# Prompt attention of a two-layer decoder step in two passes over the heads, with half of the output projection issued among the second pass

## The chip, the core and the metric

The kernel runs on one core of one Trainium2 chip. The metric is the device time of one execution in microseconds (us), taken as the median of three runs. Before the change it is 2921.13 us, and the three runs lie between 2912.52 and 2928.78 us.

A core has five engines that each work through a list of instructions of their own, in its order: PE (TensorE: matrix products, and transposes as products with an identity), DVE (VectorE), ACT (ScalarE), POOL (GpSimd) and SP, which here only issues transfers. An instruction waits at the head of its engine's list until what it needs is there, and everything behind it on that engine waits too.

## What is computed

The kernel is one inference step of a decoder of two layers: a gated linear attention layer, then a layer with differential attention, each followed by an MLP with squared ReLU. It works on a prompt of 1024 tokens (with 16 "meta" tokens ahead) and on 8 running sequences of which one token each is added ("the samples"). The change touches the attention of the prompt in the second layer and the projection behind it. Cut to that, the reference is:

```python
q, k, v = diff_project(x, w_in, pos)             # 8 heads; q and k have 2 maps of 64, v has 128
s = einsum('bqhmd,bkhmd->bhmqk', q, k) * 64**-0.5
s = where(k_pos[None, :] <= q_pos[:, None], s, -inf)
p = softmax(s, axis=-1)
a = p[:, :, 0] - lam * p[:, :, 1]                # the two maps of a head, subtracted
o = einsum('bhqk,bkhe->bqhe', a, v)
o = rms_norm(o, g_sub) * (1.0 - lam_init)        # over the 128 elements of a head
f = o.reshape(B, T, 1024) @ w_out                # w_out is 1024 x 1024
x = layer_norm(ALPHA * x + f)                    # post_norm, then the MLP
```

Everything is float32. A query sees all keys up to its own position, so that the later tokens have more keys.

## The kernel before

**Precision.** A product of two float32 matrices is made of three matmuls of a rounded type. Each operand is split into a high part and a low part: `split` (L181) copies the operand into the high part on ACT (L182) and subtracts it from the original on DVE (L183). `mm3` (L185) adds high x high, high x low and low x high (L186, L187, L188). Weights are split by `unit` and `kunit` (L162 to L179): SP loads pieces of 128 x 512 into a pool of two raw tiles, ACT rounds them into the high part (L173), GpSimd subtracts for the low part (L174). The two parts lie in the tiles `whi` and `wlo`, two of each. `kunit(w, c0)` does that for 256 columns of a 1024 x 1024 matrix, in four pieces; one such quarter of `w_out` is a unit `u`.

**Accumulators.** Results of PE go to PSUM, into three pools: `mmt` (three banks of 512 columns: the scores, `w_out`), `axt` (three banks: transposes) and `smt` (two banks: the product with V, the samples).

**Order.** Each engine's list is fixed when the kernel is built. A scheduler makes it, which takes the order in which the program issues the work as priority, and a model of the durations. So an instruction that the program issues earlier mostly stands earlier in its engine's list, but it may also be moved past others.

**Attention.** There are eight heads; a head has eight tiles of 128 queries, t = 0 to 7, and tile t has W = 16 + 128(t+1) keys.

- `prep(h)` (L1112 to L1157) makes a head's operands. It loads its 1024 keys, 1024 queries, the meta keys and the values; the raw data lie in `wlo` and `whi`, the tiles of the weights, so that two heads' are there at once. It transposes K and Q (17 transposes: one of 16 rows, eight of K, eight of Q) and splits them (four splits of 512 columns, one of 16). For every head after the first, nine transfers on GpSimd's queue (L1150 to L1156) then stack the high and the low part of each map's 64 rows, so that all 128 partitions are used and two matmuls (L1178, L1179) do the work of three; head 0 uses three (L1174 to L1176). The operands lie in half h%2 of `XH` and `XL`, the two big tiles that elsewhere hold the features of the tokens, high and low part; each half is for 512 tokens.
- `tile_(h, t)` (L1159 to L1202) computes one tile. For each map and each chunk of at most 512 keys PE makes the scores, and DVE (L1182) scales and masks them on the way out of PSUM and keeps a running row minimum (of the negated scores). ACT exponentiates (L1184) and sums; DVE combines the two maps (L1186 to L1188). PE transposes the result by 128 keys (L1197), ACT copies it out of PSUM (L1199), and PE multiplies with V (L1202) into a quarter of an `smt` bank.
- Four tiles share that bank. When it is full, ACT copies it to `Y` and squares it, and DVE sums the squares (L1239).
- `o_norm` (L1206 to L1214) normalizes finished heads, two at a time: DVE and GpSimd make the factor, and the multiplication (L1214) is GpSimd's, except for head 7, where DVE does it. `o_fm(h, c)` (L1216 to L1222) transposes head h of 512 tokens (c = 0 or 1) and splits the result into `XH` and `XL`, for `w_out`.

The loop (L1225 to L1250) runs over the heads once. `prep(h + 1)` is issued ahead of the first tile of head h, that is, one head ahead. The tiles come in the order 7, 1, 5, 3, 6, 0, 4, 2. Head 7 has 3, 2, 1, 0, 7, 6, 5, 4: after its tile 0 the first 512 tokens are finished, and `o_fm(j, 0)` for all heads j is issued ahead of its last four tiles. After the loop come `o_fm(j, 1)` and, in the next stage, eight loads of the residual (L1259 to L1261).

**Projection.** `w_out` (L882 to L908) goes through eight steps (u, c), a quarter of the columns of `w_out` for half of the tokens, in the order (0,0), (1,0), (0,1), (1,1), (2,0), (3,0), (2,1), (3,1). A step fills two accumulators, each by 48 matmuls of 256 columns, and DVE adds each to the residual in `Y` (L900). `w_out` is a generator: it hands on (`yield`) each pair of a token tile and half of its columns when it is ready, and `normalize` (L918 to L942) takes them from it, makes the layer norm and, after each half of the tokens, calls `to_fm` (L944 to L958), which transposes them for the MLP. Amid `w_out` the products of the samples (`samples`, from L1300; matmuls at L506) are issued. The MLP begins behind it (L1502).

## Time and profile before

The table is from the profiled execution, whose span, from its first to its last instruction, is 2919.7 us; the time of an execution is about 1 us more than its span. Stages are told apart by which lines run in them.

| | us |
|---|---|
| median of three runs (2912.52 to 2928.78) | 2921.13 |
| span of the profiled execution | 2919.7 |
| first row minimum of attention | 1814.3 |
| first matmul of the last group with V, and its duration | 2087.38, 1.28 |
| first matmul of the MLP | 2195.04 |
| mean granted clock of TensorE | 0.976 |

Matmuls are pipelined, and the recorded duration of one holds time in which the next is already running; the busy time of PE is therefore the time in which at least one was under way, and says nothing of how closely they follow each other. How often one can follow the next is read from the starts in a timeline. For DVE, ACT and GpSimd, busy time is time of work, except where an instruction is held up while it runs.

In the rows of groups, the columns are line, engine, operation, result and operands with their shapes and the count, then the busy time of the group and the mean ns of one instruction, then the idle time ahead of it and what ended that. In a timeline they are start, duration, engine, line and operation. In a table of stretches they are the stretch and its length, then the busy time and the number of instructions of PE, its weight loads, DVE, ACT and GpSimd, then the granted clock, the busy share of the DMA engines and GB/s.

### The profile page before, as it was taken

To read this page: it belongs to the slowest core of one execution; us is meant where nothing else is said; L and a number is where in the kernel's file an instruction comes from. 1 tells how busy PE (TensorE), PEld (TensorE's weight loads), DVE (VectorE), ACT (ScalarE), POOL (GpSimd) and SP (SyncE) were. 2 spreads that over 40 slices of the span, in tenths; PEclk is the share of its full clock that TensorE was granted. 3 is DMA by queue.
4 is the path that set the end of the run, shared out by engine and by line. 5 is a ranking of instruction groups with operands and counts; after the bars stand their busy time and mean duration, and the time that the engine had idled before them with its cause. 6 is when DMAs were issued, how large, how long until landed. Compare 5 with 4: busy or idle time off the path is not lost. (4 is left out here: it accounts for less than half of the span.)

```text
span 2919.7 us, 52085 instructions
## 1 busy us (share of the span) xinstructions
PE 2779.7 (95%) x19653; PEld 2277.6 (78%) x19653; DVE 1891.2 (65%) x2982; ACT 1044.1 (36%) x2075; POOL 1133.7 (39%) x867
## 2 busy tenths in 40 slices
PE   8889999999999999999999998889998999999997
PEld 5666767987777777777898896778888889797885
DVE  2564644457877777777667942788638855838478
ACT  3233453251222122122321112667524535335352
POOL 2230222233333334334233331132335766677664
PEclk9899999999999999999999998999999999999998
DMA  7557651514798988988387999363436778595893
GB/s 257 178 185 251 233 177 37 198 56 141 242 350 297 335 309 298 346 317 321 137 275 252 348 343 314 75 139 86 119 112 205 195 207 232 152 281 129 257 246 87
DMA packets 285366, 636.46 MB, mean 218 GB/s; under 512 B 25510, under 2 KB 141292, under 8 KB 273852
## 3 DMA queue, kind: packets, MB, share of 16 engines
q1 hardware_dynamic: 252716, 520.66, 51.6%
q0 software_dynamic: 32400, 112.50, 15.9%
q8 instruction: 154, 2.52, 0.4%
q14 instruction: 96, 0.79, 0.1%
HBM read 575.55 MB, written 44.06 MB: 212 GB/s over the span
## 5 line engine op out<-in xcount | busy, mean ns | idle before, releaser
L174 POOL TENSOR_TENSOR wlo<-raw,whi 128x512 fp32r<-128x512 f32 x256 | 360.0, 1419 | 744.0 <-ACT whi L173 670.8
L186 PE MATMUL mmt<-whi,XH 128*128 128x256 f32 (+1 forms) x1760 | 527.4, 302 | 2.9 <-ACT Y L310 2.0
L187 PE MATMUL mmt<-wlo,XH 128*128 128x256 f32 (+1 forms) x1760 | 527.8, 301 | 0.7 <-POOL wlo L174 0.7
L186 PE MATMUL mmt<-XH,whi 128*128 128x512 f32 (+1 forms) x1216 | 438.1, 361 | 7.4 <-DVE HL L183 7.2
L188 PE MATMUL mmt<-whi,XL 128*128 128x256 f32 x1536 | 437.2, 286 | 0.1
L188 PE MATMUL mmt<-XH,wlo 128*128 128x512 f32 (+1 forms) x1216 | 434.4, 358 | 0.0
L790 DVE TENSOR_REDUCE sc<-pg 128x16 f32<-128x1024 f32 x256 | 309.7, 1214 | 93.4 <-POOL pg L789 90.1
L173 ACT CAST whi<-raw 128x512 fp32r<-128x512 f32 x256 | 152.9, 619 | 578.4 <-PE mmt L188 191.1
L186 PEld LDWEIGHTS mmt<-whi,XH 128*128 128x128 f32 x1760 | 333.4, 190 | 30.1 <-issue 15.6
L187 PEld LDWEIGHTS mmt<-wlo,XH 128*128 128x128 f32 x1760 | 334.8, 190 | 28.2 <-issue 16.8
L187 PE MATMUL mmt<-XL,whi 128*128 128x512 f32 x768 | 307.3, 400 | 0.0
L188 PEld LDWEIGHTS mmt<-whi,XL 128*128 128x128 f32 x1536 | 292.1, 191 | 9.9 <-issue 8.8
L789 DVE TENSOR_TENSOR pg<-pg,qb 128x1024 f32<-128x1024 f32 x192 | 256.8, 1343 | 62.1 <-DMA pg<-in_cache_k 38.1
L186 PEld LDWEIGHTS mmt<-XH,whi 128*128 128x128 f32 x1216 | 231.7, 191 | 55.1 <-issue 13.7
L789 POOL TENSOR_TENSOR pg<-pg,qb 128x1024 f32<-128x1024 f32 x64 | 158.6, 2478 | 293.5 <-DMA pg<-in_cache_k 236.7
L188 PEld LDWEIGHTS mmt<-XH,wlo 128*128 128x128 f32 x1216 | 231.8, 191 | 35.8 <-issue 3.8
L186 PE MATMUL mmt<-whi,HH 128*128 128x512 f32 x512 | 205.6, 402 | 1.7 <-DVE Y L1014 1.7
L187 PE MATMUL mmt<-wlo,HH 128*128 128x512 f32 x512 | 204.7, 400 | 0.0
L188 PE MATMUL mmt<-whi,HL 128*128 128x512 f32 x512 | 203.9, 398 | 0.0
L187 PEld LDWEIGHTS mmt<-XL,whi 128*128 128x128 f32 x768 | 145.4, 189 | 39.6 <-issue 8.8
L1416 POOL TENSOR_TENSOR wlo<-RW,whi 128x512 fp32r<-128x512 f32 x96 | 156.3, 1749 | 37.1 <-ACT whi L1415 37.0
L1416 POOL TENSOR_TENSOR wlo<-rw,whi 128x512 fp32r<-128x512 f32 x92 | 147.7, 1674 | 41.4 <-ACT whi L1415 41.2
(441 smaller groups left out, 5769.3 us busy)
## 6 DMA issues: line engine op xcount, KB each, us to landing
pg<-in_cache_k SPq DMA_DIRECT2D x256, 512.0 KB, 6.0
pg<-in_cache_v SPq DMA_DIRECT2D x256, 512.0 KB, 6.0
XH<-xc POOLq DMA_DIRECT2D x42, 1032.0 KB, 7.9
raw<-in_mlp_w SPq DMA_DIRECT2D x164, 256.0 KB, 3.5
swt<-in_mlp_w SPq DMA_DIRECT2D x32, 1024.0 KB, 5.6
rw<-in_mlp_w SPq DMA_DIRECT2D x116, 256.0 KB, 3.8
RW<-in_mlp_w POOLq DMA_DIRECT2D x96, 256.0 KB, 6.0
xc<-XH POOLq DMA_DIRECT2D x14, 1032.0 KB, 6.8
```

What stands on the lines that cost most here:

```text
L173: S.copy(hi[:, c], raw)
L174: G.tensor_tensor(lo[:, c], raw, hi[:, c].bitcast(F32), op=ALU.subtract)
L186: TE.matmul(ps, ah, bh, start=first, stop=False)
L187: TE.matmul(ps, ah, bl, start=False, stop=False)
L188: TE.matmul(ps, al, bh, start=False, stop=last)
L789: eng.tensor_tensor(pg, pg, qb, op=ALU.mult)
L790: return V.tensor_reduce(sc[:, n, :], pg.rearrange("p (h d) -> p h d", d=64), op=ALU.add, axis=AX.X).ins
L1416: G.tensor_tensor(lo[:, k, :], t, hi[:, k, :].bitcast(F32), op=ALU.subtract)
```

## The change

The loop over the heads is run twice. The first pass computes tiles 0 to 3 of all heads, in the order 3, 1, 2, 0, and the second tiles 4 to 7, in the order 7, 5, 6, 4.

- `prep(late, h)` is called for each pass: in the first it loads 528 keys and the first 512 queries, in the second all 1040 keys, again, and the last 512 queries. In the first pass it is issued two heads ahead, in the second one head ahead. The nine transfers are now made 15 times instead of seven.
- Operands have new places (`places`): in the first pass the halves of `XH` and `XL` in turn and a new tile `opb`; in the second `XH`'s half 1 and `opb` in turn, since half 0 of `XH` and `XL` then holds the finished first 512 tokens. The low part of K has a tile of its own, `klt`. The raw data of the second pass lie in the space of `XL`'s half 1 (`araw`), so that `whi` and `wlo` are free for weights; `XL`'s half 1 is taken anew behind the last head.
- Between the passes `o_norm` and `o_fm(j, 0)` finish the first half, the residual of its tokens is loaded, and `w_out` is begun for c = 0 alone, `paced`: it stops after each accumulator. After the second tile of each head of the second pass it is taken one accumulator further, 48 matmuls and the addition on DVE. What it hands on is kept in `finished`.
- Behind the second pass a second call of `w_out` does (0,1), (1,1), (2,1), (3,1), for which the four units are loaded and split again. `both` hands the kept pairs and those of the second call to `normalize`.
- The pool of probabilities (`scp`) is as wide as the pass needs, with five tiles in the first and four in the second; `aT`'s pool is opened for each pass, with six tiles. There are three tiles of meta values instead of two. `o_norm` is called ten times instead of six, on half as many tokens.

In the lists of the engines the change makes 22 more matmuls and transposes (40 more transposes, 18 fewer score matmuls, since head 0 of the second pass uses the two-matmul form), and 135 transfers of operands on GpSimd's queue out of 63. In PE's list the 48 matmuls of a step stand together in the first head of the second pass; in the following heads they stand in pieces of 29, 7, 7 and 5, or 18, 28 and 2, between transposes and scores, and all 384 are ahead of the last product with V.

```diff
-    def w_out(w, scaled, side=None):
+    def w_out(w, scaled, side=None, order=((0, 0), (1, 0), (0, 1), (1, 1), (2, 0), (3, 0), (2, 1), (3, 1)), paced=False):
...
-        for u, c in ((0, 0), (1, 0), (0, 1), (1, 1), (2, 0), (3, 0), (2, 1), (3, 1)):
+        for u, c in order:
...
+                if paced:
+                    yield
...
+    OPW = NB * TH
+    opb = a1.tile([P, OPW], F32R, name="opb")
+    klt = a1.tile([P, NM + T], F32R, name="klt")
+    sets = [x.rearrange("p a n -> p (a n)") for x in (XH.t[0], XL.t[0], XH.t[1], XL.t[1])]
+
+    places = [sets[0], sets[1], sets[2], sets[3], sets[0], sets[1], sets[2], opb], [(sets[2], opb)[h % 2] for h in range(8)]
+    raws = []
+
+    def raw_tiles(h, late):
+
+        if not late:
+            x = wsp.tile([P, 2048], F32R, name=("whi", "wlo")[h % 2]).bitcast(F32)
+            return x[:, :512], x[:, 512:1024], x[:, 1024 : 1024 + P], x[:, 1536:]
+        if not raws:
+            raws.append(cp.tile([P, OPW], F32, name="araw", tag="XL1"))
+        x = raws[0]
+        v = 1664 + 1024 * (h % 2)
+        return x[:, :1024], x[:, 1024:1536], x[:, 1536:1664], x[:, v : v + 1024]
+
+    def prep(late, h):
+        nk = 8 if late else 4
+        w = NM + nk * P
...
-        if h == 0:
+        if h == 0 and not late:
             return vm, vx, kh_, qh_, ql_, kl_
...
-    nxt = prep(0)
-    for h in range(8):
...
+    def residual(c):
+        for u in range(4):
+            dma(Yt[:, 4 * c : 4 * c + 4, u * 256 : (u + 1) * 256], A["xres"][512 * c : 512 * c + 512, u * 256 : (u + 1) * 256].rearrange("(t p) n -> p t n", p=P))
+
+    heads = {(0, h): prep(0, h) for h in range(2)}
+    first, finished = None, []
+    for late in range(2):
+        pass_ = ExitStack()
+        scp = pass_.enter_context(tc.tile_pool(name="scp%d" % late, bufs=5 - late))
+        atp = pass_.enter_context(tc.tile_pool(name="atp%d" % late, bufs=6))
+        ts = slice(4 * late, 4 * late + 4)
+        for h in range(8):
+            head = heads.pop((late, h))
+            po = smt()
+            for n, t in enumerate((7, 5, 6, 4) if late else (3, 1, 2, 0)):
+                if n == 0:
+                    to = (1, h + 1) if late else (0, h + 2) if h < 6 else (1, 0)
+                    if to[1] < 8 and (late or h != 6):
+                        heads[to] = prep(*to)
+                tile_(h, t, po[:, t % 4 * P : (t % 4 + 1) * P], *head)
+                if late and n == 1:
+                    finished += iter(lambda: next(first, None), None)
...
+        o_norm(V, ts, slice(7, 8))
+        if late:
+            XL.t[1] = cp.tile([P, NB, TH], F32R, name="XL1", tag="XL1")
+        for j in range(8):
+            o_fm(j, late)
+        residual(late)
+        pass_.close()
+        if not late:
+            first = w_out(A["diff_w_out"][0], True, None, [(u, 0) for u in range(4)], True)
+    finished += [x for x in first if x]
     e.close()
...
+    def both():
+
+        yield from finished
+        yield from w_out(A["diff_w_out"][0], True, samples(), [(u, 1) for u in range(4)])
+
+    normalize(both(), stats, lambda c: to_fm(c, 2, xr))
```

81 lines of the change are left out of this document (27 added, 54 removed).

## The prediction

> **What bounds the kernel now.** I read the page first, then the busy time by stage, and in the attention stage the groups of instructions of each engine.
>
> ```profile
> span 2919.7 us, 52085 instructions
> PE 2779.7 (95%) x19653; PEld 2277.6 (78%) x19653; DVE 1891.2 (65%) x2982; ACT 1044.1 (36%) x2075; POOL 1133.7 (39%) x867
> ...
> 1814.00:2089.00 275.00, 247.77 (x1742) 223.71 (x1743) 223.75 (x707) 187.64 (x442) 58.28 (x69) 0.94 0.45 99
> 2089.00:2195.00 106.00, 104.84 (x795) 92.17 (x794) 40.83 (x82) 26.62 (x40) 38.92 (x27) 1.00 0.46 142
> 2195.00:2260.00 65.00, 52.79 (x405) 51.23 (x404) 54.53 (x56) 31.45 (x58) 39.28 (x36) 0.91 0.68 191
> ...
> 1876.00:1911.00 35.00, 31.07 (x205) 28.25 (x205) 29.17 (x86) 21.90 (x52) 11.23 (x11) 0.89 0.56 114
> ...
> 2008.00:2042.00 34.00, 30.65 (x227) 28.54 (x227) 31.21 (x96) 25.26 (x61) 11.13 (x11) 0.95 0.40 87
> sum 166.00, PE 149.52 PEld 136.29 DVE 142.43 ACT 116.74 POOL 42.68; mean PE 29.90 PEld 27.26 DVE 28.49 ACT 23.35 POOL 8.54
> ...
> 2160.00:2180.00 20.00, 20.00 (x172) 20.00 (x171) 11.33 (x34) 7.61 (x9) 1.39 (x2) 1.00 0.09 28
> ```
>
> The columns are the stretch, its length, and the busy time of PE, weight load, VectorE, ScalarE and GpSimd, then the granted TensorE clock and the DMA. PE is busy for 95% of the span, but a busy PE is not PE at its peak. The stretch 2160 to 2180 shows nearly only 256-column matmuls of `w_out`: 172 in 20 us, 0.116 us each, with PE busy throughout. The attention stage runs from 1814 to 2089. There the counts are lower and DVE is busy for 224 of 275 us. Between, five heads (1876 to 2042, the sum row) take 166 us, 33.2 each, of which DVE is busy 142.4/5 = 28.5. So what PE could do more is in this stage, and what else fills it is DVE. After it (2089 to 2195) PE is full and everything else is half idle: that is `w_out`. The change carries matmuls from the second stage into the first.
>
> How much of PE attention really takes is worked out from starts, because durations overlap.
>
> ```profile
> 1940.02 0.30 PE L1178 MATMUL mmt<-XH 128*128 128x320 f32 x1
> 1940.16 0.31 PE L1179 MATMUL mmt<-XH,XL 128*128 128x320 f32 x1
> 1940.31 0.35 PE L1178 MATMUL mmt<-XH 128*128 128x400 f32 x1
> ...
> 1944.78 1.06 PE L1202 MATMUL smt<-whi,aT 128*128 128x128 f32 x8
> ...
> L1202 PE MATMUL smt<-whi,aT 128*128 128x128 f32 x576 | 83.6, 283 | 0.0
> L1197 PE MATMUL axt<-c_ident,as 128*128 128x128 f32 x352 | 57.8, 292 | 11.2 <-DVE as L1188 7.1 <-DVE ast L1186 3.5 <-DVE XL L183 0.4
> L1202 PE MATMUL smt<-vm,aT 128*128 128x128 f32 x128 | 26.4, 289 | 0.2 <-ACT aT L1199 0.2
> ...
> 2087.38 1.28 PE L1202 MATMUL smt<-whi,aT 128*128 128x128 f32 x10
> ```
>
> Eight products with V take 1.06 us; less the last one's own 0.28, seven steps, 0.111 us each. Two score matmuls of 320 columns start 0.14 to 0.15 us apart, 0.45 ns a column. A head has 352/8 = 44 transposes of probabilities, (576+128)/8 = 88 matmuls with V and 17 transposes in `prep`: 149 x 0.111 = 16.5 us. Tile t has 16+128(t+1) key columns, 4736 over t = 0 to 7, times two maps, times two matmuls: 18944 x 0.45 ns = 8.5. PE is really occupied for 25 of 33.2 us. Its slack is 8 us a head, 65 in the stage, and it is not lost time in one piece: PE waits in its fixed order for DVE and the other way round.
>
> DVE by the same route:
>
> ```profile
> L1182 DVE CUSTOM_DVE_ANT_0 as<-mmt,cmask 128x272 f32<-128x272 f32 x32 | 13.6, 435 | 1.7 <-PE mmt L1179 1.6
> L1182 DVE CUSTOM_DVE_ANT_0 as<-mmt,cmask 128x464 f32<-128x464 f32 x16 | 10.1, 633 | 1.6 <-PE mmt L1179 1.2 <-PE mmt L1176 0.4
> L1188 DVE SCALAR_TENSOR_TENSOR as<-as,ast 128x1040 f32<-128x1040 f32 x8 | 10.4, 1295 | 0.0
> L1188 DVE SCALAR_TENSOR_TENSOR as<-as,ast 128x272 f32<-128x272 f32 x8 | 3.9, 493 | 0.0
> L1187 DVE TENSOR_SCALAR ast<-ast,ls,lamv 128x1 f32<-128x1 f32 x64 | 17.3, 271 | 0.7
> L1186 DVE RECIPROCAL ast<-ls 128x1 f32<-128x1 f32 x64 | 10.1, 159 | 5.1 <-ACT as L1184 4.7
> L183 DVE TENSOR_TENSOR XL<-axt,XH 128x512 fp32r<-128x512 f32 x24 | 16.2, 684 | 0.2 <-ACT XH L182 0.2
> L183 DVE TENSOR_TENSOR XL<-axt,XH 128x16 fp32r<-128x16 f32 x6 | 1.0, 164 | 0.0
> L1239 DVE TENSOR_REDUCE oss<-smt 128x4 f32<-128x512 f32 x15 | 10.3, 686 | 0.0
> L900 DVE TENSOR_TENSOR Y<-Y,mmt 128x512 f32<-128x512 f32 x1 | 0.7, 689 | 9.0 <-PE mmt L188 9.0
> ...
> L1188 DVE SCALAR_TENSOR_TENSOR as<-as,ast 128x528 f32<-128x528 f32 x8 | 18.3, 2290 | 0.1
> ```
>
> From 272 and 464 columns, the row-minimum pass (L1182) costs 0.155 us and 1.03 ns a column; the combination (L1188), from 272 and 1040, 0.21 us and 1.04 ns a column. Tiles 0 to 3 have 1344 columns and 10 chunks: 2 x 1344 x 1.03 ns + 10 x 0.155 + 1344 x 1.04 ns + 4 x 0.21 + 4 x (0.271+0.159) = 8.3 us. Tiles 4 to 7 have 3392 columns and 18 chunks: 15.9. With four splits of 512, one of 16 and two sums of squares a head is 24.2 + 2.7 + 0.2 + 1.4 = 28.5, which is what the windows count. So a head takes 1.165 times the work of its fullest engine (33.2/28.5): that factor is the friction of the fixed order.
>
> **The change part by part.** The sum is against the profiled execution, span 2919.7 and a time 1 us or so longer; the median of the three runs is 2921.13.
>
> *Early pass* (tiles 0 to 3, eight heads). DVE: 8.3 + two splits of 512, one of 16, one sum of squares = 8.3 + 1.4 + 0.2 + 0.7 = 10.5 us a head. PE: (14+28+9) x 0.111 + 1344 x 4 x 0.45 ns = 8.1. DVE bounds it. With the friction of now, 10.5 x 1.165 = 12.2; 98 for eight. Lower end 10.5 (84), upper end from the moves, below.
>
> *Late pass*. DVE: 15.9 + three splits of 512 and one of 16 (all 1040 keys again, 512 queries) + 0.7 + 0.7 for the residual addition of `w_out` (L900) = 19.5. PE: (30+60+13) x 0.111 + 3392 x 4 x 0.45 ns + 48 matmuls of `w_out` x 0.116 = 11.4 + 6.1 + 5.6 = 23.1. So PE becomes the fullest engine here. If the 48 matmuls only fill what PE would wait anyway, a head takes 23.1; with the friction of now, 23.1 x 1.165 = 26.9. In the issue order of the changed program the 48 stand in pieces (29, 7, 7, 5 in one head, 18, 28, 2 in the next) beside the splits of the next head's `prep`, which give DVE work of its own, so part of the friction is covered; but L900 is queued on DVE ahead of the row minima of tile 6 and waits for the last piece, and ScalarE's exponentials and the transposes wait behind those. I take the middle, 25.0; 200 for eight.
>
> *What is paid twice.* Half of the K splits (528 columns a head) is the price of the two passes, 8 x (0.684+0.164) = 6.8 us of DVE and 40 more transposes (4.4 us of PE); both are in the sums above.
>
> *Start and change of pass.* The low halves of K go to `opb` and `klt`, whose space the last pages of the decode hold; two splits of 512 and two of 16 (1.7 us) that lay ahead of the stage now lie in it. Between 0 and 5, I take 2. At the change of pass stand the 32 transposes of `o_fm(j, 0)`, 3.6 us of PE; now they lie in head 7. So attention takes 2 + 98 + 200 + 4 = 304 us from 1814 instead of the 274.7 to the last product with V (2087.38+1.28 = 2088.7): **+30**.
>
> *The tail.* Now 690 matmuls of `w_out` are left there:
>
> ```profile
> L186 PE MATMUL mmt<-whi,XH 128*128 128x256 f32 x230 | 65.2, 287 | 0.5 <-ACT whi L173 0.5
> L506 PE MATMUL smt<-rw,zoT 128*32 128x512 f32 x32 | 13.4, 604 | 0.0
> ```
>
> The group of L186 counts 230, its two sisters as many. Afterwards 384 are left: (690-384) x 0.116 = 36 us less. The products of the samples (L506) stay. The first half no longer fills PE while `o_norm` and `o_fm` of the second half run, so 1 to 5 us come back, I take 3: **-33**. The second half of `w_out` loads and splits its four units again, which GpSimd does in 4 x 1.4 us a unit against 96 x 0.116 = 11 us of PE; that is hidden, and costs 5 us a unit if it isn't.
>
> *After the tail* (2195 to 2260) DVE is busy 54.5 of 65 us; the first half's norm now comes earlier, but the second half's comes last as before: 0 to -4, I take -1.
>
> *GpSimd.* While it works on SBUF, DVE's combination stands still:
>
> ```profile
> 1899.28 4.73 DVE L1188 SCALAR_TENSOR_TENSOR as<-as,ast 128x528 f32<-128x528 f32 x1
> ...
> 1899.78 3.65 POOL L1214 TENSOR_TENSOR Y<-Y,orr 128x2048 f32<-128x2048 f32 x1
> ...
> L1214 POOL TENSOR_TENSOR Y<-Y,orr 128x2048 f32<-128x2048 f32 x3 | 11.0, 3653 | 0.0
> L174 POOL TENSOR_TENSOR wlo<-raw,whi 128x512 fp32r<-128x512 f32 x4 | 5.4, 1361 | 15.0 <-ACT whi L173 15.0
> ...
> 1925.01 0.51 POOL L1150 DMA_DIRECT2D XH<-XH  x1 [17.59 <-ACT XH L182]
> 1940.18 0.51 POOL L1156 DMA_DIRECT2D XL<-XL  x1 [2.44 <-DMA XL<-XL]
> ...
> q0 software_dynamic: 4839, 15.91, 29.3%
> ```
>
> The combination of 528 columns took 4.73 us beside the 3.65 us of L1214, and its mean is 2.29, where the line through 272 and 1040 columns gives 0.76: 8 x 1.5 = 12 us of DVE lost in the stage. The multiplications of L1214 keep their elements; 16 more splits of weights (L174, 1.36 us) come in, 22 us. At the rate of now (12 lost beside 11.0 + 5.4 of these two groups) that is up to 16 us of DVE, 2 a late head: 21.5 of 23.1, still not the bound, so nothing is added, and the upper end is 2 x 8 = 16. The Trainium skill, SBUF — State Buffer, section "SBUF: two separate sides", calls the port pair of the two engines an exclusive lock for a DVE operation with two SBUF inputs against a GpSimd operation that reads SBUF; the rows above agree. By that rule alone, each new microsecond of GpSimd would hold such an operation for its length, and the sum would be up to 16 longer, 2933.
>
> **Sum:** +30 - 33 - 1 = -4, **2917 us**: no change that can be told from none. A measurement of this kernel tells 0.5%, 15 us.
>
> **Rivals.** *Hidden fully.* The 48 matmuls cost a late head nothing over 23.1, and the early pass runs at 11.3, since its operands are ready two heads ahead: 90 + 185 instead of 298, so -27 and 2894 or so. For it: the splits beside the matmuls, and that 1.165 contains waits for late operands. Against: one accumulator of three is held by `w_out`.
>
> *Slower: the matmuls stand in the way.* PE's order is fixed. If DVE and ScalarE run out of work while 29 or 48 matmuls stand ahead of the next scores, the late head takes what it would without them (DVE 19.5 x 1.165 = 22.7) plus all 5.6: 28.3, 226 in all: +26, 2943. It decides from a late head of 25.5 on (zero) and 27.4 (0.5% slower). For it: L900's place, and that DVE now waits for scores (L1182) most. Against: the pieces.
>
> *The moves bound the early pass.* Nine moves of operands a head go through GpSimd's queue: 15.2 us from first to last issue (1925.01 to 1940.18), and 29.3% of 275 us over six heads, 13.4 us of DMA a head. The early pass has half the bytes, 6.7 us, but as many moves. If the number counts, 13.4 a head instead of 12.2: +10, 2927. The Trainium skill, DMA: Bandwidth & Descriptors, section "Anatomy of one DMA — SWDGE (gpsimd) path", gives about 2.0 us fixed and the rest by size; by that a half-size move saves little.
>
> *The change doesn't do what it says:* the first half's matmuls pile up behind the pass. The issue order has all eight steps ahead of the last products with V, so this is kept at 0.02; the first half would fill the tail again, and the late head without it takes 22.7: +30 - 8 x 2.3 = +12, 2933.
>
> **How the numbers follow.** Forecast 0.42 (2903 to 2931), hidden fully 0.25, in the way 0.25, the moves 0.06, not done 0.02. Faster by over 0.5% (under 2906): most of the second and a sixth of the first, 0.32; slower (over 2936): most of the third and a little of the others, 0.28; within, 0.40. The range goes down to the lower rival with the early pass, the start and the time after the tail at their lower ends (-6, -2, -3: 2883), and up to the slower one with 12 of the 16 us of the port (2955).
>
> **What would show it.** Early heads near 12 us apart and late ones near 25 (by the sums of squares, one a head); DVE busy about 85% in the early pass and 78% in the late one; L900 waiting for PE 1 us or so each; the stretch from the last product with V to the first matmul of the MLP near 73 us instead of 106. Late heads at 28 mean the third case, at 23 the second. I am wrong altogether if a wait that no row of now shows appears at the change of pass.

## The result, and the profile after

The changed kernel takes 2942.19 us (median of five runs, 2940.64 to 2949.22) against 2921.13 before: the ratio is 1.0073, with a 95% interval of 1.0054 to 1.0092. It is slower by 0.7%. The forecast was 2917, no change, in a range of 2883 to 2955. The profiled execution is the slowest of the five: its span is 2947.5, 27.8 more than that of before, while the medians differ by 21.

The page of the changed kernel, and the busy time of the four stages (the columns are as before: stretch, length, PE, weight load, DVE, ACT, GpSimd, granted clock, DMA share, GB/s):

```profile
span 2947.5 us, 52508 instructions
PE 2786.2 (95%) x19675; PEld 2282.9 (77%) x19675; DVE 1889.1 (64%) x3006; ACT 1061.3 (36%) x2107; POOL 1189.7 (40%) x964
...
1819.44:1932.95 113.51, 94.62 (x600) 84.52 (x599) 81.73 (x305) 77.64 (x219) 58.33 (x87) 0.84 0.77 163
1932.95:2146.26 213.31, 199.02 (x1493) 187.10 (x1492) 153.24 (x438) 131.64 (x263) 68.73 (x89) 0.98 0.53 118
2146.26:2231.32 85.06, 70.03 (x495) 58.49 (x492) 42.67 (x82) 27.73 (x41) 39.49 (x27) 0.92 0.56 166
2231.32:2297.00 65.68, 61.43 (x477) 60.91 (x478) 59.62 (x58) 32.58 (x59) 39.55 (x38) 0.93 0.86 258
```

The bounds of the stages are four events, here in the timelines of DVE and PE: the first row minimum, the first row minimum of a second-pass tile (352 columns), the last product with V, the first matmul of the MLP. With them stand the first and the last sum of squares of each pass, eight in each.

```profile
1819.44 0.44 DVE L1197 CUSTOM_DVE_ANT_0 as<-mmt,cmask 128x272 f32<-128x272 f32 x1 [0.29 <-PE mmt L1191]
...
1838.22 0.69 DVE L1263 TENSOR_REDUCE oss<-smt 128x4 f32<-128x512 f32 x1
...
1928.10 0.68 DVE L1263 TENSOR_REDUCE oss<-smt 128x4 f32<-128x512 f32 x1
...
1932.95 0.53 DVE L1197 CUSTOM_DVE_ANT_0 as<-mmt,cmask 128x352 f32<-128x352 f32 x1 [0.93 <-PE mmt L1194]
...
1966.65 0.68 DVE L1263 TENSOR_REDUCE oss<-smt 128x4 f32<-128x512 f32 x1
...
2148.34 0.68 DVE L1263 TENSOR_REDUCE oss<-smt 128x4 f32<-128x512 f32 x1
```

```profile
1932.48 0.74 PE L1194 MATMUL mmt<-XH 128*128 128x352 f32 x3 [2.26 <-DMA XH<-XH]
...
2145.65 0.61 PE L1217 MATMUL smt<-araw,aT 128*128 128x128 f32 x4
...
2229.25 0.90 PE L951 MATMUL axt<-c_ident,Y 128*128 128x128 f32 x3 [9.73 <-ACT Y L940]
...
2231.32 1.01 PE L186 MATMUL mmt<-XH,whi 128*128 128x258 f32 x3
```

The first line of PE is the wait that ends last ahead of the second pass: 2.26 us for a transfer of the new head's operands.

All later runs are read by the same four events. In us:

| kernel | ratio to before (95%) | first pass | second pass | attention | to the MLP | after that |
|---|---|---|---|---|---|---|
| before | | | | 274.4 | 105.9 | 725.1 |
| the change | 1.0073 (1.0054 to 1.0092) | 113.5 | 213.3 | 326.8 | 85.1 | 716.2 |
| e1 w_out whole | 1.0108 (1.0089 to 1.0126) | 114.0 | 195.0 | 309.0 | 107.5 | 725.1 |
| e2 samples first | 1.0084 (1.0063 to 1.0104) | 114.2 | 214.4 | 328.6 | 80.3 | 720.6 |
| e3 no transfers in the first pass | 1.0071 (1.0052 to 1.0091) | 101.7 | 222.4 | 324.1 | 83.3 | 717.4 |
| e4 transfers made, not used | 1.0145 (1.0116 to 1.0174) | 124.2 | 215.2 | 339.3 | 82.6 | 716.4 |
| e5 before, tiles by size | 1.0013 (0.9996 to 1.0029) | | | 276.3 | 104.1 | 725.8 |
| e6 no transfers at all, w_out whole | 1.0074 (1.0055 to 1.0093) | 96.9 | 195.5 | 292.4 | 107.1 | 730.8 |
| e7 as e4, small transfers | 1.0080 (1.0061 to 1.0100) | 108.7 | 221.0 | 329.7 | 86.0 | 715.0 |
| e8 as e3, step after the fourth tile | 1.0155 (1.0135 to 1.0175) | 105.6 | 245.4 | 351.0 | 82.4 | 716.5 |
| e9 the change, more work for PE | 1.0116 (1.0099 to 1.0132) | 112.6 | 220.3 | 332.9 | 83.4 | 714.7 |
| e10 as e4, more work for PE | 1.0161 (1.0147 to 1.0175) | 118.4 | 217.7 | 336.0 | 86.1 | 716.6 |
| e11 the change, half steps | 1.0083 (1.0068 to 1.0097) | 110.3 | 213.2 | 323.5 | 85.9 | 715.7 |
| e12 as e3, half steps | 1.0021 (1.0009 to 1.0033) | 105.2 | 207.7 | 312.9 | 85.9 | 715.5 |
| e13 as e3, w_out whole | 1.0062 (1.0043 to 1.0080) | 103.8 | 190.5 | 294.2 | 107.0 | 729.8 |
| e14 before, K twice | 1.0040 (1.0023 to 1.0056) | | | 285.1 | 104.1 | 723.4 |
| e15 the change, third raw tile | 1.0097 (1.0073 to 1.0122) | 108.8 | 227.1 | 335.8 | 86.2 | 714.2 |
| e16 as e12, third raw tile | 1.0029 (1.0013 to 1.0046) | 105.3 | 208.6 | 314.0 | 85.1 | 718.4 |

The ratios are the better comparison, since before itself measured 2917.3 to 2921.9 beside these runs. The stage times are of one profiled execution each, and differences of a few us between single runs say little: the first pass without transfers, with the same text, took 96.9 to 105.6 us (e3, e6, e8, e12, e13). (Before, the first matmul of the MLP starts at 2194.56; the 2195.04 given above is the fifth.) When attention begins (1802 to 1824) hangs on the decode ahead of it and differs between executions, so a span is not the sum of this row alone. Against before, the change loses 52.4 us in attention (326.8 - 274.4) and 5.1 at its start, and gains 20.8 in the stage of w_out and 8.9 behind it. The matmuls that were to move did move, and the stage of w_out is shorter. Attention pays more than that.

What DVE and PE waited for in the first pass (group, count, busy time and mean, then the idle time ahead of it and what ended it):

```profile
L1197 DVE CUSTOM_DVE_ANT_0 as<-mmt,cmask 128x272 f32<-128x272 f32 (+2 forms) x64 | 26.8, 434 | 19.5 <-PE mmt L1194 18.6 <-PE mmt L1191 0.8
```

```profile
L1212 PE MATMUL axt<-c_ident,as 128*128 128x128 f32 x112 | 23.6, 341 | 9.7 <-DVE klt L183 5.3 <-DVE orr L1227 2.7 <-DVE ast L1201 0.9
```

DVE, which I had as the bound of this pass, is busy for 81.7 of 113.5 us, 72% where I had 85, and stands 19.5 us ahead of row minima for scores. In the second pass it is busy for 153.2 of 213.3, again 72%, where I had 78.

### The profile page after: what moved, and what is told of

Read it like the earlier page. It is cut to its first block, busy times and chain, and to the rows that moved or that the text cites. A ratio compares the mean times of both kernels' runs of the same rounds, so it can differ in the third digit from the quotient of the medians.

```text
span 2947.5 us, 52508 instructions
## 1 busy us (share of the span) xinstructions
PE 2786.2 (95%) x19675; PEld 2282.9 (77%) x19675; DVE 1889.1 (64%) x3006; ACT 1061.3 (36%) x2107; POOL 1189.7 (40%) x964
## 4 chain that ended last, share of the span: by engine, by line
PE 68%; DMA 12%; DVE 9%; issue 5%; POOL 4%; ACT 2%; SPq 1%; POOLq 0%; DVEq 0%; ACTq 0%
PE mmt L186 16%; PE mmt L187 16%; PE mmt L188 16%; PE smt L830 4%; PE axt L186 2%; PE axt L187 2%; PE axt L188 2%; DMA XH<-xc 2%; PE smt L1217 1%; DMA rw<-in_mlp_w 1%; DMA swt<-in_mlp_w 1%; DVE Y L972 1%; POOL wlo L174 1%; DVE pg L789 1%; POOL wlo L1445 1%
## 5 line engine op out<-in xcount | busy, mean ns | idle before, releaser
L174 POOL TENSOR_TENSOR wlo<-raw,whi 128x512 fp32r<-128x512 f32 x272 | 381.0, 1419 | 732.0 <-ACT whi L173 672.8
L173 ACT CAST whi<-raw 128x512 fp32r<-128x512 f32 x272 | 162.4, 619 | 569.0 <-PE mmt L188 201.8
L187 PEld LDWEIGHTS mmt<-wlo,XH 128*128 128x128 f32 x1760 | 334.0, 190 | 26.7 <-issue 15.1
```

The source lines that it names most:

```text
L173: S.copy(hi[:, c], raw)
L174: G.tensor_tensor(lo[:, c], raw, hi[:, c].bitcast(F32), op=ALU.subtract)
L187: TE.matmul(ps, ah, bl, start=False, stop=False)
```

## The experiments

**e1: the two passes, w_out whole.** The paced call and its use are taken out, and w_out runs behind the second pass in its old order.

```diff
-        if not late:
-            first = w_out(A["diff_w_out"][0], True, None, [(u, 0) for u in range(4)], True)
-    finished += [x for x in first if x]
...
-                if late and n == 1:
-                    finished += iter(lambda: next(first, None), None)
...
-        yield from finished
-        yield from w_out(A["diff_w_out"][0], True, samples(), [(u, 1) for u in range(4)])
+        yield from w_out(A["diff_w_out"][0], True, samples())
```

> The changed kernel with its two passes, but w_out kept whole behind the second pass, in the order it had before the change (all 768 matmuls in the tail). Theory 'the 48 matmuls mostly stand in the way': a late head falls from the 26.0 us that the changed kernel shows to 22 or less (4 or more of the 5.6 us of matmuls were paid for), the late pass gets 30 us or more shorter, the tail 36 longer by the matmuls and some 9 shorter because the samples end earlier: 2935 to 2945, the same as the changed kernel's 2942. Theory 'they are mostly hidden and the two passes themselves cost': a late head stays at 24 to 26, the time is 2955 to 2970. My own forecast had 22.7 a head here.

It took 2951.4 us, 1.0108. The second pass is 18.3 us shorter than in the change (213.3 - 195.0), 2.3 a head on average: of 5.6 us of matmuls 3.3 are hidden and 2.3 paid. In return w_out and what follows are 31.3 us longer (832.6 against 801.3). So dealing out is worth 13 us by the stages, and 0.35% by the ratios, 10 us. Neither theory had it: the first had the matmuls paid for nearly in full, the second the time of 2955 or more. What stands out is the attention without any dealing: 309.0 against 274.4. The loss is in the passes. Where in them, the sums of squares show, the first and the last of each pass, of e1 and below of e13 (no transfers in the first pass, see there):

```profile
1828.23 0.69 DVE L1261 TENSOR_REDUCE oss<-smt 128x4 f32<-128x512 f32 x1
...
1919.06 0.68 DVE L1261 TENSOR_REDUCE oss<-smt 128x4 f32<-128x512 f32 x1
...
1960.46 0.69 DVE L1261 TENSOR_REDUCE oss<-smt 128x4 f32<-128x512 f32 x1
...
2119.53 0.68 DVE L1261 TENSOR_REDUCE oss<-smt 128x4 f32<-128x512 f32 x1
```

```profile
1833.52 0.69 DVE L1261 TENSOR_REDUCE oss<-smt 128x4 f32<-128x512 f32 x1
...
1912.62 0.68 DVE L1261 TENSOR_REDUCE oss<-smt 128x4 f32<-128x512 f32 x1
...
1954.82 0.68 DVE L1261 TENSOR_REDUCE oss<-smt 128x4 f32<-128x512 f32 x1
...
2109.69 0.68 DVE L1261 TENSOR_REDUCE oss<-smt 128x4 f32<-128x512 f32 x1
```

In us, with the first row minimum of each run (1819.44, 1808.59, 1813.37):

| | the sum | the change | e1 | e13 |
|---|---|---|---|---|
| first row minimum to first sum of squares | 12.2 | 18.8 | 19.6 | 20.2 |
| seven more heads of the first pass, each | 12.2 | 12.8 | 13.0 | 11.3 |
| last sum of the first pass to first of the second | 29.0, or 26.7 without matmuls | 38.5 | 41.4 | 42.2 |
| seven more heads of the second pass, each | 25.0, or 22.7 without matmuls | 26.0 | 22.7 | 22.1 |

The sum had 4 us at the change of pass, which stand in its third row. Without the dealt matmuls, the heads of the second pass stand as far apart as forecast. What is longer is the beginning of each pass.

**e5: before, with the tiles of a head by size.**

```diff
-        for n, t in enumerate((3, 2, 1, 0, 7, 6, 5, 4) if h == 7 else (7, 1, 5, 3, 6, 0, 4, 2)):
+        for n, t in enumerate((3, 2, 1, 0, 7, 6, 5, 4) if h == 7 else (7, 5, 6, 4, 3, 1, 2, 0)):
...
-            at = t % 4 if h == 7 else t // 2
+            at = t % 4
...
-                ts = (slice(0, 4), slice(4, 8))[n // 4] if h == 7 else slice(t % 2, 8, 2)
+                ts = slice(0, 4) if t < 4 else slice(4, 8)
```

> The kernel before, one pass, with nothing changed but the order of a head's tiles: 7, 5, 6, 4, 3, 1, 2, 0 instead of 7, 1, 5, 3, 6, 0, 4, 2 (head 7 as it was). With w_out kept whole, the two passes took 24.4 us a late head, and 12.7 an early one where no transfer is waited for: 37.1, less 0.85 us of K splits that are made twice, 36.2 against 33.2. Theory 'large tiles run worse with no small ones between them': the order alone costs 2 to 3 us a head, 2932 to 2942. Rival 'what each pass does anew (loads, preparation, transfers) is what costs': 2915 to 2924, as before.

2924.71 us, 1.0013 (0.9996 to 1.0029): no difference beyond the uncertainty, and attention takes 276.3 instead of 274.4. That large tiles stand together is not the cause; that fell.

**e14: before, with the K work of half the keys done twice.** In `prep` the first 528 keys are loaded, transposed and split a second time, into a tile that nothing reads.

```diff
+        k2x = vk[:, 1280:1792].rearrange("p (t d) -> p t d", d=P)
+        dma(k2x, kr[NM : NM + 512].rearrange("(t p) d -> p t d", p=P))
...
+        ps = axt()
+        TE.transpose(ps[:, :NM], km, ident[:NM, :NM])
+        split(again[:, 0, :NM], again[:, 1, :NM], ps[:, :NM])
+        ps = axt()
+        for i in range(4):
+            TE.transpose(ps[:, i * P : (i + 1) * P], k2x[:, i, :], ident)
+        split(again[:, 0, NM:], again[:, 1, NM:], ps)
```

> The kernel before, with the loads, transposes and splits of the first 528 keys of each head made a second time, into a tile that nothing reads: 8 x (0.85 us of DVE + 0.56 of PE + 0.7 of ACT) and nothing else of the two passes. Theory 'what is paid twice is paid in full, times the friction': 8 to 12 us slower than before. Rival 'it fits into idle time': -3 to +4.

2931.9 us, 1.0040 (1.0023 to 1.0056), 11.7 us at the level of before; attention takes 10.7 us more. The work that the two passes do twice is paid in full, and with friction: 6.8 us of DVE, with their loads and transposes, cost 10.7.

**e13 and e3: no transfers in the first pass.** All heads of the first pass use the three-matmul form; the low part of K goes where the second map's operand would be. In e13 w_out is whole as in e1, in e3 it is dealt out as in the change.

```diff
-        kl_ = (klt if late or h else opb)[:, :w]
+        kl_ = klt[:, :w] if late else k2[1] if h else opb[:, :w]
...
-        if h == 0 and not late:
+        if not late:
             return vm, vx, kh_, qh_, ql_, kl_
```

> The changed kernel, with the scores of all heads of the first pass made by three matmuls of 64 rows, as head 0 does it, so that the 63 transfers of operands on GpSimd's queue fall away in the first pass; PE gets 1.2 us a head more. Theory 'the transfers pace the first pass': an early head falls from 12.8 us to 10.5 to 11.5, the first pass from 113.5 to 95 to 103: 10 to 18 us faster than 2942, 2924 to 2932. Rival 'the order of PE and DVE paces it': 12.5 to 13.5 a head, no gain or up to 5 us slower.

> The two passes with w_out kept whole behind them and no transfers in the first pass; the second pass as in the change. First pass 97 to 102, second 193 to 198: 2936 to 2942. It is the base for the price of the dealt matmuls without the transfers of the first pass: against the run without transfers with steps of 48 (late pass 222) and with half steps (208). Theory 'steps of 48 cost a late head half of their 5.6 us, half steps a third': late pass 195 here. Rival 'the second pass takes 205 or more whatever is dealt into it': 205 or more.

With w_out whole, 2939.85 instead of 2951.4: the transfers of the first pass cost 14.8 us of attention (309.0 - 294.2), 10.2 of them in the first pass itself. Their removal in the dealt-out kernel shortens the first pass as expected (101.7), but the second pass takes 222.4 instead of 213.3, so that the time stays (2940.27): the same 48 matmuls a head now cost 31.9 us (222.4 - 190.5) where they cost 18.3 with the transfers. Without the transfers, then, dealing the steps out gains nothing (1.0071 against 1.0062). I had not expected that the two are not independent. The text of the second pass is the same; in the lists that the scheduler makes, the pieces stand elsewhere.

```profile
1808.64:1922.61 113.97, 95.80 (x600) 85.56 (x599) 80.81 (x305) 77.91 (x219) 58.28 (x87) 0.83 0.75 162
1922.61:2117.61 195.00, 169.41 (x1152) 148.72 (x1153) 144.76 (x432) 119.73 (x245) 48.36 (x73) 0.96 0.50 108
```

```profile
1813.37:1917.16 103.79, 96.31 (x662) 80.29 (x661) 83.67 (x301) 76.52 (x216) 26.37 (x24) 0.93 0.37 99
1917.16:2107.61 190.45, 164.84 (x1158) 145.57 (x1157) 143.11 (x430) 120.62 (x247) 48.98 (x73) 0.97 0.50 109
```

The first rows are e1's two passes, the second e13's. In the first pass the granted clock rises from 0.83 to 0.93 and the DMA share falls from 0.75 to 0.37. DVE's work is the same within 3 us; what goes is waiting.

**e6: no transfers in either pass, w_out whole.**

```diff
-        kl_ = (klt if late or h else opb)[:, :w]
+        kl_ = k2[1] if late or h else opb[:, :w]
...
-        if h == 0 and not late:
-            return vm, vx, kh_, qh_, ql_, kl_
+        return vm, vx, kh_, qh_, ql_, kl_
```

> The two passes with w_out kept whole behind them (2951), and the scores of all heads in both passes by three matmuls of 64 rows, so that no transfer of operands on GpSimd's queue is left; PE gets 3 us more a late head (20.5 in all). The early pass gets 12 us shorter, as in the run without its transfers. Theory 'late heads wait for their operands': a late head falls from 24.4 to 21.5 to 22.7, the time is 2916 to 2928. Rival 'the chain from scores to product with V sets a late head': 24 to 25.5, 2935 to 2945.

2941.36. The second pass takes 195.5, with three-matmul scores and no transfer to wait for, as against 195.0 with transfers. As a forecast of the time the theory of late operands in the second pass fell. But the beginning of that pass gets shorter: its first row minimum starts at 1909.16, ahead of the last sum of squares of the first pass (1912.36), where it came 4.5 us behind it in e13 (1917.16 and 1912.62), and from that sum to the next it is 34.9 us instead of 42.2. The seven heads that follow stand 22.8 apart instead of 22.1, and most of the gain is lost again. So at its beginning the second pass does wait for operands that the transfers make; whether PE's added work alone takes the gain back is not shown.

**e4, e7, e10: what of the transfers costs.** In e4 the scores are those of e3, and the 63 transfers are made all the same, to places that nothing reads. In e7 each has 64 columns instead of 512 or 528. e10 is e4 with 128 transposes of a constant, as in e9 below.

```diff
+        if not late:
+            d = at[:, 2 * w + 2048 : 3 * w + 2048]
+            move(d[64:], kh_[64:])
+            move(d[:64], kl_[:64])
+            move(d[64:], kl_[64:])
+            for a, b in (q2, ql2):
+                move(b[64:], a[64:])
+                move(b[:64], a[64:])
+                move(b[64:], a[:64])
+            return vm, vx, kh_, qh_, ql_, kl_
```

> As the kernel whose first pass uses three matmuls of 64 rows, but the 63 transfers are made all the same, to places that no matmul reads: their queue and their bytes stay, and no score waits for them. Theory 'waiting for the transfers is what costs': as fast as the kernel without them, 2924 to 2932. Rival 'their bytes cost, beside the loads, or what stands behind them in GpSimd's queue': the gain is lost, 2938 to 2945.

> As the kernel that makes the 63 transfers of the first pass to places that nothing reads (2958, first pass 124 us), but each of 64 columns instead of 512 or 528: as many transfers, packets and waits in GpSimd's queue, an eighth of the bytes. Theory 'their bytes, on DMA engines that the loads of this pass fill already, are the cost': first pass 102 to 107, 2940 to 2946. Rival 'their number or GpSimd's queue': first pass 117 to 126, 2951 to 2962.

> The kernel with unused full-size transfers in the first pass (2958; first pass 124 us, in which the clock stood at 0.50 for 24 us on end), with the same 128 added transposes. Theory 'the clock made the difference between it and the kernel with small transfers': first pass 108 or less, 2942 or less. Rival 'the bytes did': 122 to 130.

e4 took 2958.23, e7 2942.55, e10 2964.29. No score waits for these transfers, and they still cost: the first pass takes 124.2 us with the full ones, 108.7 with the small ones, 101.7 without any. So most of the price goes with the size. The loads show one way in which they may act. In the rows of the DMA issues of the first pass, the last column is the median time from issue to landing; the row is the load of V of every other head, in the change, in e3, in e7 and in e4:

```profile
wlo<-out_v_rows_p SPq DMA_DIRECT2D x2, 256.0 KB, 7.8
```

```profile
wlo<-out_v_rows_p SPq DMA_DIRECT2D x2, 256.0 KB, 3.3
```

```profile
wlo<-out_v_rows_p SPq DMA_DIRECT2D x2, 256.0 KB, 3.4
```

```profile
wlo<-out_v_rows_p SPq DMA_DIRECT2D x2, 256.0 KB, 8.9
```

7.8 and 8.9 us beside the full transfers, 3.3 without any and 3.4 beside the small ones, in a row of two loads each. But with the same full transfers in e9 (below) it is 4.8, and the first pass is hardly shorter than in the change, so that this alone does not set its length. The granted clock differs too: in e4 it stood at 0.50 from 1841 to 1865, and e10 was to tell whether that is the whole difference. Its clock is 0.93, its first pass 118.4, of which up to 14.2 are the added transposes. That lies between the two forecasts, and e10's time is not below e4's: how much of the price is the clock and how much the loads stays open.

**e9: more work for PE in the first pass.**

```diff
                 tile_(h, t, po[:, t % 4 * P : (t % 4 + 1) * P], *head)
+                if not late:
+                    ps = axt()
+                    for i in range(4):
+                        TE.transpose(ps[:, i * P : (i + 1) * P], ident, ident)
```

> The changed kernel with four transposes of a constant added after each tile of the first pass, whose result nothing reads: 128 in all, 14 us of PE's time for nothing. In the changed kernel the granted clock is 0.84 over the first pass: it falls to 0.50 for 4 us or so after most stretches in which PE idled. Theory 'PE has so little to do in the first pass that its clock falls, and that makes it the bound': with more to do the clock rises to 0.92 or more and the pass stays at 113 or gets up to 8 us shorter, in spite of the added work. Rival 'the transfers alone set the pass': the clock may rise, the pass stays at 113 to 118. Rival 'the pass is bound by PE's order': it gets 8 to 14 us longer, 2950 to 2956.

2947.74. The granted clock of the first pass rises from 0.84 to 0.90, a little short of what the first theory asks, and the pass takes 112.6 instead of 113.5 with 14 us of PE work added. So the third theory, with 8 to 14 us more, fell: on balance the added work costs nothing there, whether because PE has the room or because the higher clock pays for it. Nothing is won either, and the first two theories are not told apart. The second pass is 7 us longer with the same text, and the time with it.

**e15: a third tile for raw data.** SP issues a head's loads in the order K, Q, V, and V waits until the products of the head that holds the tile are done; the next loads stand behind it.

```diff
-            x = wsp.tile([P, 2048], F32R, name=("whi", "wlo")[h % 2]).bitcast(F32)
+            x = r3p.tile([P, 2048], F32, name="raw3") if h % 3 == 2 else wsp.tile([P, 2048], F32R, name=("whi", "wlo")[h % 3]).bitcast(F32)
```

> The changed kernel with a third tile for the raw data of the first pass, so that a head's loads do not stand on SP's queue behind those of V that wait 52 us in all for the last products of the head that holds the tile. Theory 'late loads make the transfers late': first pass 103 to 108 instead of 113.5, 2930 to 2937. Rival 'the transfers cost by themselves': 111 to 116, 2939 to 2946.

2950.52: slower. The first pass takes 108.8, 4.7 less, a part of what late loads would explain; the second pass takes 227.1, 13.8 more, with the same text. Late loads explain at most that part of the first pass; as a forecast of the time the run was a miss.

**e8, e11, e12, e16: where and how the matmuls are dealt in.** e8 is e3 with the step after a head's fourth tile (`if late and n == 3`). e11 is the change with steps of 24 matmuls, each with its own addition, after the first and the third tile; e12 is the same on e3; e16 is e12 with the third raw tile.

```diff
+            if paced:
+                for t0 in range(4 * c, 4 * c + 4):
+                    ps = mmt()[:, :256]
+                    a = slice(t0 * P, (t0 + 1) * P)
+                    for k in range(NB):
+                        mm3(ps, XH[:, k, a], XL[:, k, a], hv[:, k, :], lv[:, k, :], k == 0, k == NB - 1)
+                    yv = Yt[:, t0, u * 256 : (u + 1) * 256]
+                    V.tensor_tensor(yv, yv, ps, op=ALU.add)
...
-                if late and n == 1:
+                if late and n in (0, 2):
```

> The changed kernel without the transfers of the first pass (2940; late pass 222 us), with each step of 48 matmuls of w_out issued after a late head's fourth tile instead of its second. Theory 'PE is idle where the scores of the next head wait for its transfers (5.9 us recorded for one half of the heads), and matmuls there would fill it': late pass 207 to 215, 2926 to 2934. Rival 'a step costs the same wherever it stands': 218 to 226, 2936 to 2945.

> The changed kernel with the first half of w_out in steps of 24 matmuls (one token tile, 256 columns), each with its own addition, one after the first and one after the third tile of each late head, instead of 48 after the second. Theory 'a step costs because DVE stands at its addition (1.77 us each, 14.1 in all) and an accumulator is held': late pass 200 to 208 instead of 213, 2929 to 2937. Rival 'PE, with 23.1 us of work in a late head of 26, sets the pass, however the matmuls are cut': 211 to 217, 2939 to 2946.

> Both: no transfers in the first pass, and half steps. If each helps by itself as forecast (first pass 102, late pass 205): 2922 to 2930, level with the kernel before or a little behind. If the late pass stays at 215 to 222: 2934 to 2942.

> All three: no transfers in the first pass, half steps of w_out, a third raw tile. If loads still hold the first pass up: 99 to 103 instead of 105, 2919 to 2924, level with the kernel before; otherwise as without the third tile, 2924 to 2928.

e8 took 2963.4, e11 2941.09, e12 2925.39, e16 2930.83. The additions and the row minima among DVE's groups in the second pass, for the change, e3, e8 and e12 in turn:

```profile
L1197 DVE CUSTOM_DVE_ANT_0 as<-mmt,cmask 128x352 f32<-128x352 f32 (+3 forms) x64 | 35.7, 557 | 17.4 <-PE mmt L1194 17.1
L900 DVE TENSOR_TENSOR Y<-Y,mmt 128x512 f32<-128x512 f32 x8 | 5.5, 688 | 14.1 <-PE mmt L188 14.1
```

```profile
L900 DVE TENSOR_TENSOR Y<-Y,mmt 128x512 f32<-128x512 f32 x8 | 5.5, 687 | 15.5 <-PE mmt L188 15.5
```

```profile
L900 DVE TENSOR_TENSOR Y<-Y,mmt 128x512 f32<-128x512 f32 x8 | 5.5, 689 | 68.3 <-PE mmt L188 68.3
```

```profile
L1209 DVE CUSTOM_DVE_ANT_0 as<-mmt,cmask 128x352 f32<-128x352 f32 (+3 forms) x64 | 35.1, 557 | 7.3 <-PE mmt L1206 7.3
L897 DVE TENSOR_TENSOR Y<-Y,mmt 128x256 f32<-128x256 f32 x16 | 6.7, 418 | 3.5 <-PE mmt L188 3.0 <-DMA araw<-out_k_rows_p 0.3
```

DVE waits 14.1 us for eight additions in the change, 15.5 in e3, 68.3 in e8, and 3.5 for sixteen of half the size in e12. Against e13's 190.5, the 384 matmuls cost 31.9 us in e3, 54.9 in e8 and 17.2 in e12. So the place of a step and its size decide its price, and both of e8's theories fell: it is neither the same everywhere, nor does PE's idle time at the end of a head pay for it. DVE's wait goes with the price among e3, e8 and e12; between the change (18.3) and e3 (31.9) it is about the same, so that it isn't all of it. But half steps alone, with the transfers left in (e11), gave nothing, as the rival had it: 213.2 against 213.3. So e12's time, though it lies within what was expected, does not show that each edit helps by itself. e12 has the best time of the two-pass kernels, 0.2% above before (1.0009 to 1.0033); none is below it. A third raw tile added nothing to it, and e16 came out above both of its forecasts.

**e2: the samples ahead of the second half of w_out.**

```diff
-        yield from finished
-        yield from w_out(A["diff_w_out"][0], True, samples(), [(u, 1) for u in range(4)])
+        next(samples())
+        yield from finished
+        yield from w_out(A["diff_w_out"][0], True, None, [(u, 1) for u in range(4)])
```

> The changed kernel with the products of the samples issued ahead of the second half of w_out, instead of in the middle of it. Theory 'the samples end the tail': their results are copied beside the prompt's into the operands of the MLP, and in the changed kernel that copy comes at 2228.3, 1.3 us after the last matmul of w_out plus 10; issued earlier, PE no longer idles 9.7 us ahead of the MLP: 8 to 12 us faster than 2942, 2930 to 2934. Rival 'the norm of the second half ends the tail': the MLP waits for the last layer norm anyhow, 0 to 3 us faster.

2944.91: no gain. The idle time of 9.7 us ahead of the MLP (the row at 2229.25 above) is mostly gone, the stage takes 80.3 instead of 85.1, and the MLP and what follows take 4.4 more. The gain is given back later; where, I did not follow. The theory of the samples is right on the wait and wrong on the time.

## Why the prediction was wrong

The sum was +30 - 33 - 1. In the profiled execution it is +57.6 to the last product with V (2146.26 against 2088.7), -20.8 and -8.9 (the two last stages).

- **The beginning of each pass was left out.** This is the step that failed: attention as 98 + 200 + 4, that is, every head at the distance that heads have amid the stage, 4 us for the change of pass and nothing more for the first head of a pass. By it, attention in two passes without dealing would take 283.6 from the first row minimum (98 + 8 x 22.7 + 4); e1 shows 309.0. Of these 25.4 us, 22.1 lie at the two beginnings: 19.6 + 41.4 = 61.0 where the sum has 12.2 + 26.7 = 38.9. Taking the transfers out of the first pass (e13) leaves 10.6 of the 25.4, but the beginnings stay as long (62.4): it is the heads between that get quicker. The first pass begins with a granted clock of 0.65 in e1 (0.68 in the change). At the change of pass, the first row minimum of a head comes 3.5 us after the sum of squares of the head before (4.9 in the change, 1932.95 after 1928.10), while between later heads of the second pass in e1 it comes 8.5 to 14.4 us ahead of it: the overlap of two heads is lost there. Part of that is operands that come late (e6; the wait of 2.26 us in the change); the rest is the chain that fills anew beside `o_norm` and `o_fm`, which no run isolates. It is the place that I had named as the sign of being wrong altogether. The kernel before has such a cost too: its attention takes 274.4, 8.8 more than eight heads of 33.2, and I took the 274.7 as a whole on one side of the sum and heads alone on the other.
- **The friction held between the heads.** 1.165 gave 12.2 and 22.7 (the latter with the addition of w_out, 0.7, in it); e1 shows 13.0 and 22.7, and e13, without the transfers of the first pass, 11.3 and 22.1. The K work that is done twice costs more than the 6.8 x 1.165 = 8 that the sum had for it, 10.7 by e14, but this did not make the late heads longer than forecast.
- **The dealing out was right in its total.** Forecast: a late head of 25.0 with the 48 matmuls and 22.7 without, 2.3 a head paid, 18.4 in all. Measured: 18.3 (213.3 against e1's 195.0). The tail and what is behind it: forecast 34 less, measured 29.7 less than before and 31.3 less than e1. The matmuls do fill waits. That the total came out so close is partly chance: the seven later heads pay 3.2 each (26.0 against 22.7), the beginning of the pass takes 2.9 less with the matmuls than without, and without the first pass's transfers the same steps cost 31.9 (e3).
- **The rival of the transfers was right in kind and too small.** I gave it 13.4 us a head in place of 12.2, +10 in all, and a chance of 0.06, since an early head has half the bytes and is prepared two heads ahead. The cost is 14.8 of attention, 11.7 of it in the seven early heads (13.0 against 11.3 each), and it is not mainly that the number of transfers sets a pace: with e7's small ones, to places that nothing reads, the first pass takes 108.7, with full ones 124.2. Their size counts, in a pass in which the loads come more thickly too (DMA share 0.77 in the row of the first pass, 0.45 in the stage before).
- **The rival with the forecast time was not the cause.** "The matmuls stand in the way", 28.3 a head, gave 2943 and came within 1 us of the median, for another reason: the late heads stand 26.0 apart (1966.65 to 2148.34, seven heads), not 28.3, and the rest lies at the beginnings of the passes. The wait that it names is there: DVE waits 14.1 us at L900, 1.77 each, where I had "1 us or so". e8, with 54.9 us paid for 44.8 of matmuls, shows a case in which they stand in the way in full.
- **Start and tail.** 5.1 later at the first row minimum, where I had 2; the start differs between executions by more than that. From the last product with V to the MLP it is 85.1 us, not 73, although PE is busy for only 70.0 of it: PE idles 9.7 us ahead of the MLP, for the samples and the last norm (e2). Most of that came back behind it: 8.9 less where I had 1.
- **GpSimd's port** was rightly left out of the sum. The two widths of DVE's combination that took most beyond their line, in the change:

```profile
L1203 DVE SCALAR_TENSOR_TENSOR as<-as,ast 128x912 f32<-128x912 f32 x8 | 13.7, 1714 | 0.1
L1203 DVE SCALAR_TENSOR_TENSOR as<-as,ast 128x272 f32<-128x272 f32 x8 | 6.6, 830 | 0.0
```

By the line of 0.21 us and 1.04 ns a column they lose 8 x (0.55 + 0.34) = 7 us, less than the 12 that 528 columns alone lost before. The rule by which the sum would have been 16 longer did not come to bear: GpSimd has more to do, and DVE lost less.

## What to carry to other kernels

A factor of friction that is measured between heads amid a stage says nothing of how the stage begins. When a loop is cut into two passes, give each pass a beginning of its own (here 61 us for the two where the heads' distance gave 39), and work that every pass does anew at least the price of the stage's bound (here 10.7 us for 6.8 of DVE). Work dealt into a busy stage has no price of its own: the same 384 matmuls cost 17 to 55 us by their place and piece size, so look first at the instruction that takes them over on another engine. And where a scheduler makes the lists, an edit in one stage moves the next: second passes of the same text took 213 to 227 us, so judge an edit by its stage and by the whole time.

## What the runs showed of the hardware that I had not expected

**The clock of TensorE falls after short idle stretches too.** In stretches of 1 us in the first pass of the change:

```profile
1862.00:1863.00 1.00, 0.89 (x8) 0.65 (x7) 1.00 (x3) 1.00 (x5) 0.98 (x2) 1.00 0.06 10
1863.00:1864.00 1.00, 0.00 (x0) 0.00 (x0) 1.00 (x1) 0.84 (x2) 1.00 (x1) 1.00 0.52 148
1864.00:1865.00 1.00, 0.08 (x1) 0.08 (x2) 1.00 (x5) 0.00 (x0) 0.83 (x2) 1.00 1.16 342
1865.00:1866.00 1.00, 0.58 (x4) 0.34 (x4) 0.96 (x3) 0.39 (x1) 0.00 (x0) 0.77 1.06 294
1866.00:1867.00 1.00, 0.53 (x3) 0.56 (x4) 1.00 (x4) 0.74 (x3) 0.38 (x1) 0.50 0.86 242
1867.00:1868.00 1.00, 1.00 (x7) 1.00 (x7) 1.00 (x3) 0.21 (x1) 1.00 (x3) 0.50 1.26 327
...
1871.00:1872.00 1.00, 1.00 (x6) 1.00 (x6) 0.45 (x2) 0.10 (x1) 0.00 (x0) 0.50 1.29 259
1872.00:1873.00 1.00, 1.00 (x8) 0.85 (x6) 0.00 (x0) 0.27 (x1) 0.00 (x0) 0.82 1.37 286
```

PE was idle for about 2 us, then busy for half of the next two; the clock fell to 0.50 amid the stretch from 1865 and came back in that from 1872, with PE busy throughout from 1867 on. The Trainium skill, TensorE: Matmul & The Clock Gate, section "Part 1: The HAM clock gate (the "warmup" mystery)", has the array at half rate after an idle window of about 3.4 us and at full rate after a busy one; here 2 us nearly without a matmul, in 4 of little work, were enough for the fall, and the way back took 5 us of full work. In the trace's record of the clock the changes about this place stand at 1841.64, 1845.06, 1865.54, 1872.36 and 1882.60, each a multiple of 3.4 us after the one before, and in the 3.4 us that end at 1865.54 PE was busy for 1.37. That fits a clock that is set anew every 3.4 us by what PE did in them; no run tests it. At the start of the pass the way back was longer:

```profile
1817.80:1831.20 13.40, 13.37 (x57) 10.61 (x56) 9.80 (x37) 8.50 (x24) 9.39 (x18) 0.50 0.69 152
```

PE is recorded busy throughout, and the clock stays at 0.50.

In e4 the clock fell with PE recorded busy:

```profile
1838.00:1839.00 1.00, 1.00 (x11) 0.88 (x10) 0.89 (x6) 1.00 (x4) 0.90 (x2) 1.00 0.74 216
1839.00:1840.00 1.00, 0.94 (x8) 0.70 (x6) 1.00 (x5) 1.00 (x4) 0.81 (x3) 1.00 1.31 290
1840.00:1841.00 1.00, 1.00 (x7) 0.76 (x6) 1.00 (x4) 1.00 (x5) 0.83 (x2) 0.89 1.42 202
1841.00:1842.00 1.00, 1.00 (x6) 1.00 (x6) 1.00 (x8) 0.79 (x3) 0.00 (x0) 0.50 1.40 204
...
1852.00:1866.00 14.00, 14.00 (x62) 11.49 (x61) 6.21 (x26) 5.92 (x17) 6.14 (x10) 0.55 0.66 131
```

No idle time explains that stretch of some 24 us at 0.50; what started it is open, and so is what kept the clock down at the start of the pass.
